# Recurrence gates as two tiles on row halves of the tensor array

## Chip, cores and metric

The kernel runs on one NeuronCore of a Trainium2 chip. What counts is the device time of one execution in microseconds (us). Before the change the median of three runs was 2362.04 us (2358.81 to 2364.02).

## The reference

Two layers over 1024 latent tokens and 256 context tokens of width 1024. Each layer normalises and modulates its input, projects it (`w_in`) and runs three branches of width 512: windowed attention, a Conformer convolution of 31 taps, and a recurrence (RG-LRU) in both directions. Each branch is multiplied by a SiLU gate, projected by `w_branch`, weighted by a sigmoid gate (`w_gate`), summed, and projected by `w_out`; a norm closes the layer. The change touches the recurrence's two gates only:

```python
def block_diag_linear(x, w, b):            # w: (8 blocks, 64, 64)
    xb = x.reshape(x.shape[:-1] + (LRU_BLOCKS, LRU_BLOCK_DIM))
    return jnp.einsum('btnd,nde->btne', xb, w).reshape(x.shape) + b

def rglru_inputs(x, w_a, b_a, w_x, b_x, lam):
    r = jax.nn.sigmoid(block_diag_linear(x, w_a, b_a))
    i = jax.nn.sigmoid(block_diag_linear(x, w_x, b_x))
    log_a = -LRU_C * r * jax.nn.softplus(-lam)
    a = jnp.exp(log_a)
    u = jnp.sqrt(-jnp.expm1(2.0 * log_a)) * i * x
    return a, u
```

## The kernel before

Channels lie on partitions and tokens along the free axis. Every product keeps fp32 accuracy by splitting both operands into a rounded part and a rest (`split`: a copy on ACT, a subtraction on DVE) in the type fp32r, and summing three products: high by high, high by low, low by high. Tokens come in three stretches: the context (256) and two halves of the latent tokens (512 each). In the gates of the recurrence the context stretch is 260 wide.

`phase1` does everything up to the gated branch outputs, `phase2` the branch and output projections and the norm. In `phase1` nine generators run as streams: `lru`, `att_values`, `att_scores`, `lru_in`, `lru_out`, `att_proj`, `att_out`, `conv` and `gates` (the `w_gate` products, not the gates of the recurrence). A `Driver` merges them: each `yield` ends a stage and names the engine that the next one needs and a condition; the driver keeps an estimated clock for PE, ACT and DVE, fed by `pe_cost` (columns of a product, whatever its rows), `act_cost` and `dve_cost`, and picks among the stages that should be ready by priority. `lru` has priority 0 in layer 0 and 1 in layer 1. The tile framework then orders the instructions of each engine by a simulated timeline and sets the waits.

For each of four blocks of 128 channels `lru_in` loads the gate weights (lines 588 to 595), makes the input projection, and splits the weights. A block of 128 channels is two of the reference's blocks of 64, so a gate's 64x64 matrices stand on the diagonal of a 128x128 tile that a memset on POOL has filled with zeros. Two directions and two gates make a tile of 128x512. In `lru`, for each channel block and direction, `taps` makes the short convolution on DVE, `parts` splits it into `xh` and `xl`, and `gate(dr, gi)` (lines 640 to 650) runs one gate: for each stretch three products over all 128 rows into one bank of PSUM, and one tanh on ACT with the bias column out of `drv`. The two gates are two stages. Then come `decay`, `drive`, `root` and `scan`. When the second direction of the last block begins, `state["late"]` lets `att_scores` start.

Banks for products come from a pool of four (`psum`); `pl_` counts those that the other streams' products hold, and lets at most three be held while the recurrence runs. The gates of the recurrence are not counted there. Wide products of `gates` use a second pool (`psum2`) until the recurrence has ended.

`load_params` and `derive_params` bring the biases to columns: `drv` holds 0.5 times the bias, columns 0 to 7 for the first gate and 8 to 15 for the second, by direction and channel block.

Of the kernel before, what the change touches and what calls it, by code (L numbers as in the profile page):

```python
# [35 lines left out]
NS, NHF, NW, NWL, NXP, NYY = 10, 14, 4, 2, 7, 6  # L36
LH = 6

# Orders the merged streams, by phase and by layer.
LEAD = (2.0, 3.0, 1.5, 2.0)  # L40
SLACK = (1.0, 5.0, 2.0, 2.0)
MARGIN = (1.0, 3.0, 1.5, 0.0)
# [7 lines left out]


class Meter:
    """An engine, with an estimate of the time that the instructions given to it take."""

    def __init__(self, eng, cost):
        self.eng, self.cost, self.t = eng, cost, 0.0
# [46 lines left out]


class Driver:
    """Merges streams of work into one order for each engine: a stage goes out when what it waits for should be there."""

    def __init__(self, pe, act, dve):
        self.phase = 0
# [1 line left out]
        self.t = dict(pe=0.0, act=0.0, dve=0.0)  # L111

    def side(self, fn):
        """Work that waits for nothing but a load."""
        was = {e: m.t for e, m in self.eng.items()}
        r = fn()
        end = self.t["pe"]
        for e, m in self.eng.items():
            d = m.t - was[e]
            if d:  # L120
                self.t[e] = max(self.t[e], min(self.t["pe"] + 2.0, self.t[e] + 2.0)) + d
                end = max(end, self.t[e])
            m.t = was[e]
        return r, end
# [19 lines left out]
        return nxt  # L144

    def run(self, gens, prio, until=None, live=()):
        """Runs the streams to their end, or to that of one of them, and returns those that are left."""
        live = list(live)
        for i, g in enumerate(gens):
            s = dict(gen=g, kind="pe", ready=self.t["pe"], prio=prio[i], cond=None)  # L150
            if self.advance(s, next(g, None)):
                live.append(s)
        while live and (until is None or any(s["gen"] is until for s in live)):
            open_ = [s for s in live if s["cond"] is None or s["cond"]()]
            assert open_, "every stream waits"
            tp = self.t["pe"]
            pick = None
            side = [s for s in open_ if s["kind"] != "pe" and self.t[s["kind"]] < tp + LEAD[self.phase]
                    and s["ready"] < max(tp, self.t[s["kind"]]) + SLACK[self.phase]]
            if side:  # L160
                pick = min(side, key=lambda s: s["prio"])
            else:
                main = [s for s in open_ if s["kind"] == "pe"]
                now = [s for s in main if s["ready"] + MARGIN[self.phase] <= tp]
                if now:
                    pick = min(now, key=lambda s: s["prio"])
                else:
                    pick = min(open_, key=lambda s: (max(s["ready"], self.t[s["kind"]]), s["prio"]))
            if not self.advance(pick, self.step(pick)):
                live.remove(pick)  # L170
        return live
# [18 lines left out]
def kernel(  # L190
# [51 lines left out]
    xs_d = DR.tile([T, D], F32, tag="xs", name="xs_d")  # L242

    P_ADA, P_GATE, P_CB, P_CG, P_CLB, P_LCW, P_LCB, P_BA, P_BX, P_LAM = 0, 24, 48, 52, 56, 60, 92, 100, 108, 116
    prm, cwt, drv = [], [], []

    def load_rows(l, get):
        ra, rb = get(), get()
# [29 lines left out]
    def derive_params(l):  # L278
        p = prm[l]
        d = K.tile([128, 64], F32, tag=f"drv{l}", name=f"drv{l}")  # L280
        dve.tensor_scalar(out=d[:, 0:16], in0=p[:, P_BA:P_BA + 16], scalar1=0.5, scalar2=None, op0=ALU.mult)
        dve.tensor_scalar(out=d[:, 16:40], in0=p[:, P_GATE:P_GATE + 24], scalar1=0.5, scalar2=None, op0=ALU.mult)
        dve.tensor_scalar(out=d[:, 40:48], in0=p[:, P_CG:P_CG + 8], scalar1=0.5, scalar2=None, op0=ALU.mult)
        t = SM.tile([128, 48], F32, tag="sp", name="sp_t")
        y, e, sx, s2, r, ny = (t[:, 8 * i:8 * i + 8] for i in range(6))
        dve.tensor_scalar(out=y, in0=p[:, P_LAM:P_LAM + 8], scalar1=-1.0, scalar2=None, op0=ALU.mult)
        dve.tensor_tensor(out=ny, in0=p[:, P_LAM:P_LAM + 8], in1=y, op=ALU.max)
        act.activation(out=e, in_=ny, func=AF.Exp, scale=-1.0)
        dve.tensor_scalar(out=r, in0=e, scalar1=2.0, scalar2=None, op0=ALU.add)
        dve.reciprocal(out=r, in_=r)  # L290
        dve.tensor_tensor(out=sx, in0=e, in1=r, op=ALU.mult)
        dve.tensor_tensor(out=s2, in0=sx, in1=sx, op=ALU.mult)
        dve.tensor_scalar(out=r, in0=s2, scalar1=1.0 / 19, scalar2=1.0 / 17, op0=ALU.mult, op1=ALU.add)
        for k in (15, 13, 11, 9, 7, 5, 3, 1):
            dve.tensor_tensor(out=r, in0=r, in1=s2, op=ALU.mult)
            dve.tensor_scalar(out=r, in0=r, scalar1=1.0 / k, scalar2=None, op0=ALU.add)
        dve.tensor_tensor(out=r, in0=r, in1=sx, op=ALU.mult)
        dve.tensor_scalar(out=y, in0=y, scalar1=0.0, scalar2=None, op0=ALU.max)
        dve.scalar_tensor_tensor(out=r, in0=r, scalar=2.0, in1=y, op0=ALU.mult, op1=ALU.add)
        dve.tensor_scalar(out=d[:, 48:56], in0=r, scalar1=-4.0, scalar2=None, op0=ALU.mult)  # L300
        dve.tensor_scalar(out=d[:, 56:64], in0=r, scalar1=4.0, scalar2=None, op0=ALU.mult)
        drv.append(d)

    sink = K.tile([128, DEPTH * NH], F32, tag="sink", name="sink")
# [4 lines left out]
    wlive = [0]  # L309

    class Wt:
        """A unit of weights, split into two parts; held from its load to its last product."""

        def __init__(self, src, a, b):
            wlive[0] += 1
# [45 lines left out]
    ada = {}  # L361

    def ada_fin(l, jjs, ps, rows, r):
        """Rows of ada, still in PSUM, to its columns, with the bias."""
        n = len(jjs) * 128
        act.activation(out=r[0:rows, 0:n], in_=ps[0:rows, 0:n], func=AF.Copy)
        for i in range(len(jjs)):
# [8 lines left out]
            dve.tensor_scalar(out=dst, in0=dst, scalar1=0.25, scalar2=None, op0=ALU.mult)  # L376

    def ada_pair(l, jj, row):
        """Two columns of ada, in three of the four products of the parts and the fourth."""
        ws = [Wt(w_ada[l][i * 512:i * 512 + 512, jj * 128:jj * 128 + 256].rearrange("(k p) n -> p k n", p=128), 4, 256)  # L380
              for i in range(2)]
        ps = psum()
        for k in range(KD):
            for v in range(2):
                pe.matmul(out=ps[0:4, 0:256], lhsT=csr[:, k, :], rhs=ws[k // 4][v][:, k % 4, :],
                          start=(k == 0 and v == 0), stop=(k == KD - 1 and v == 1))
        ada_fin(l, [jj, jj + 1], ps, 4, row)
        for w in ws:
            w.free()
# [99 lines left out]
                norm_x(*v)  # L489

    class Pool_:
        """Counts what is held of a pool, in the order of emission."""

        def __init__(self, n):
            self.n, self.used = n, 0
# [14 lines left out]
    def phase1(l, R, RH):  # L510
# [11 lines left out]
        def half(name, dt=F32):  # L522
            return RH.tile([128, 512], dt, tag="h", name=name, bufs=NHF)
# [58 lines left out]
        def lru_in():  # L582
            for cc in range(4):
# [1 line left out]
                w = wcols(w_in[l], O_XL + cc * 128)  # L585
                sl.take()
                hl_.take(3)
                lw_raw = half("lw_raw")
                pool.memset(lw_raw, 0.0)
                for dr in range(2):  # L590
                    for gi, wsrc in enumerate((lru_w_a, lru_w_x)):
                        o = (dr * 2 + gi) * 128
                        for e in range(2):
                            sp.dma_start(out=lw_raw[64 * e:64 * e + 64, o + 64 * e:o + 64 * e + 64],
                                           in_=wsrc[l, dr, 2 * cc + e])
                X = slot("X")
                for a, e in ((0, XL_C), (XL_C + C, XL_L), (XL_L + S, XW)):
                    pool.memset(X[:, a:e], 0.0)
# [6 lines left out]
                    yield from gemm_nt(w, nt, evac)  # L605
                w.free()
                yield "act"
                lwh, lwl = half("lwh", F32R), half("lwl", F32R)
                split(lw_raw, lwh, lwl)
                hl_.give()  # L610
                lws[cc] = (lwh, lwl)
# [2 lines left out]
        def lru():  # L614
            for cc in range(4):
# [17 lines left out]
                    v["xh", dr], v["xl", dr] = slot("xh", F32R)[:, 0:CW], slot("xl", F32R)[:, 0:CW]  # L633
                    split(v["xc", dr], v["xh", dr], v["xl", dr])

                def gate(dr, gi):
                    dst = v["AI"[gi], dr] = slot("AI"[gi])[:, 0:CW]
                    b = gi * 8 + dr * 4 + cc
                    wo = (dr * 2 + gi) * 128
                    for ti, t0, n in allt:  # L640
                        o, n = (0, CL) if ti == 0 else (CL + t0 - C, n)
                        ps = psum()
                        for j, (a, r) in enumerate(((lwh, "xh"), (lwh, "xl"), (lwl, "xh"))):
                            pe.matmul(out=ps[:, 0:n], lhsT=a[:, wo:wo + 128], rhs=v[r, dr][:, o:o + n], start=(j == 0),
                                      stop=(j == 2))
                        act.activation(out=dst[:, o:o + n], in_=ps[:, 0:n], func=AF.Tanh, scale=0.5, bias=d[:, b:b + 1])

                def decay(dr):
                    i = dr * 4 + cc
# [29 lines left out]
                parts(0)  # L679
                yield ("pe", sl.room(2))  # L680
                sl.take(2)
                gate(0, 0)
                yield "pe"
                gate(0, 1)
                sl.give(2)
                yield ("dve", sl.room())
                sl.take()
# [18 lines left out]
                sl.give(3)  # L706
                yield ("pe", sl.room(2))
                sl.take(2)
                gate(1, 0)
                yield "pe"  # L710
                gate(1, 1)
                hl_.give(2)
                sl.give(2)
                yield ("act", sl.room(2))
# [406 lines left out]
    def phase2(l, R, RH):  # L1121
# [175 lines left out]
                done.add(ti)  # L1297

        def hdst(ti):
            """Whether there is room for what the next layer takes in."""  # L1300
            return ti in done if ti == 0 else hq.room()() and (ti == 1 or 1 in done and 2 in done)

        def norm():
# [131 lines left out]
```

## Time and profile before

| | |
|---|---|
| median of three runs | 2362.04 us |
| span of the profiled execution | 2360.6 us |
| PE busy | 2300.4 us, 97% |
| weight loads (PEld) busy | 1931.6 us, 82% |
| DVE busy | 1762.1 us, 75% |
| ACT busy | 1063.9 us, 45% |
| POOL busy | 88.1 us, 4% |
| DMA moved | 309.94 MB, 131 GB/s |
| granted TensorE clock, mean | 0.993 of 2.4 GHz |

The profile is one execution. A product's recorded time is longer than its share of the engine, since products follow each other before the one ahead has ended; the starts in the timeline show the pace. Names such as `ps<-xh,lwh` give the output and the operands; `128*128` are rows and columns of weights in use, then follow the shape that streams through and the count. The gate products of the recurrence are those with `lwh` or `lwl`.

### The profile page before, as it was taken

The page shows a single profiled execution, that of the slowest core. Times are in us where ns is not written, and L with a number is a line of the kernel's source. Part 1 is how long each engine was busy: PE and PEld are TensorE (multiplying, and loading weights), DVE is VectorE, ACT ScalarE, POOL GpSimd, SP SyncE. Part 2 cuts the span into 40 slices and gives each one's busy share as a digit, 9 for nine tenths or more (in the row PEclk, how much of TensorE's full clock was granted, in tenths as well). Part 3 has the DMA queues.
Part 4 walks back from the last instruction along what each step waited for, and adds up shares of the span by engine and source line. Part 5 has one row for each costly group of instructions (what it writes and reads, how often), then busy time and mean ns, then how long its engine had stood idle before and what let it go on. Part 6 is the DMA issues. An engine that isn't in the chain of part 4 may idle for free.

```text
span 2360.6 us, 32714 instructions
## 1 busy us (share of the span) xinstructions
PE 2300.4 (97%) x12477; PEld 1931.6 (82%) x12477; DVE 1762.1 (75%) x2589; ACT 1063.9 (45%) x1702; POOL 88.1 (4%) x135
## 2 busy tenths in 40 slices
PE   7999999999999999999999999999999999999998
PEld 3888888878888887888888888888888878778988
DVE  5579868758969775448888839979687887667786
ACT  4555453245444565323445535555343456443231
POOL 1000000000000011000101000000000011000000
PEclk8999999999999999999999999999999999999999
DMA  7222324433344223466565521223433334338482
GB/s 276 68 74 96 116 76 132 135 102 105 96 134 126 88 87 99 169 226 215 176 210 184 188 60 61 83 90 130 134 96 95 98 95 129 119 128 273 136 274 73
DMA packets 305821, 309.94 MB, mean 131 GB/s; under 512 B 20608, under 2 KB 239616, under 8 KB 305664
## 3 DMA queue, kind: packets, MB, share of 16 engines
q1 hardware_dynamic: 277152, 255.94, 34.2%
q10 hardware_dynamic: 28512, 51.92, 6.1%
q8 instruction: 98, 1.61, 0.3%
q14 instruction: 59, 0.48, 0.1%
HBM read 232.92 MB, written 74.87 MB: 130 GB/s over the span
## 4 chain that ended last, share of the span: by engine, by line
PE 89%; DVE 4%; ACT 3%; DMA 2%; issue 1%; SPq 0%; POOLq 0%; POOL 0%; ACTq 0%; DVEq 0%
PE ps L73 82%; PE yp L73 3%; PE pt L73 2%; PE pa L73 1%; DVE wlo L73 1%; ACT whi L73 1%; DMA thl<-th 1%; DVE mx L73 0%; DMA qd<-qd 0%; DMA raw<-in_w_ada_dram 0%; DVE xp L73 0%; DVE pl L73 0%; PE p L73 0%; DMA raw<-in_w_in_dram 0%; DVE P L73 0%
## 5 line engine op out<-in xcount | busy, mean ns | idle before, releaser
L73 PE MATMUL ps<-hlhi,whi 128*128 128x512 f32 x1728 | 682.8, 396 | 4.6 <-ACT tg L73 2.1
L73 PE MATMUL ps<-hllo,whi 128*128 128x512 f32 x1728 | 678.5, 393 | 0.1
L73 PE MATMUL ps<-hlhi,wlo 128*128 128x512 f32 x1728 | 676.3, 392 | 1.1 <-DVE wlo L73 1.1
L73 ACT ACTIVATE whi<-raw 128x1024 fp32r<-128x1024 f32 x240 | 253.8, 1059 | 454.8 <-PE ps L73 425.8
L73 DVE TENSOR_TENSOR wlo<-raw,whi 128x1024 fp32r<-128x1024 f32 x240 | 293.4, 1223 | 143.0 <-ACT whi L73 142.3
L73 PEld LDWEIGHTS ps<-hlhi,whi 128*128 128x128 f32 x1728 | 325.3, 188 | 71.5 <-ACT tg L73 3.5
L73 PEld LDWEIGHTS ps<-hlhi,wlo 128*128 128x128 f32 x1728 | 325.1, 188 | 70.5 <-DVE wlo L73 2.0
L73 PEld LDWEIGHTS ps<-hllo,whi 128*128 128x128 f32 x1728 | 325.5, 188 | 63.7 <-issue 0.7
L73 DVE SCALAR_TENSOR_TENSOR acc<-u,cwt,acc 128x1296 f32<-128x1296 f32 (+1 forms) x240 | 342.1, 1426 | 2.2
L73 PE MATMUL ps<-yh,whi 128*128 128x512 f32 (+1 forms) x480 | 177.8, 377 | 8.5 <-DVE thl L73 6.5
L73 PE MATMUL ps<-yl,whi 128*128 128x512 f32 (+1 forms) x480 | 178.1, 373 | 1.5 <-DVE yl L73 1.5
L73 PE MATMUL ps<-yh,wlo 128*128 128x512 f32 (+1 forms) x480 | 179.0, 374 | 0.0
L73 ACT ACTIVATE ph<-pt 128x512 fp32r<-128x512 f32 x160 | 94.3, 594 | 162.2 <-PE pt L73 158.3
L73 DVE TENSOR_REDUCE mx<-ps 128x1 f32<-128x640 f32 (+2 forms) x144 | 104.6, 744 | 62.3 <-PE ps L73 61.8
L73 PE MATMUL ps<-whi,hlhi 128*128 128x256 f32 x512 | 144.3, 284 | 0.0
L73 PE MATMUL ps<-wlo,hlhi 128*128 128x256 f32 x512 | 144.0, 283 | 0.0
L73 ACT ACTIVATE P<-ps,nm 128x640 f32<-128x640 f32 (+2 forms) x144 | 104.9, 733 | 85.9 <-DVE nm L73 82.0
L73 DVE TENSOR_TENSOR pl<-pt,ph 128x512 fp32r<-128x512 f32 x160 | 108.7, 684 | 46.7 <-ACT ph L73 44.3
L73 PE MATMUL ps<-whi,hllo 128*128 128x256 f32 x512 | 142.6, 283 | 0.0
L73 PE MATMUL ps<-hchi,whi 128*128 128x256 f32 x480 | 138.1, 288 | 3.6 <-ACT rstd L73 1.2
L73 PE MATMUL ps<-hchi,wlo 128*128 128x256 f32 x480 | 137.4, 286 | 0.0
L73 PE MATMUL ps<-hclo,whi 128*128 128x256 f32 x480 | 136.5, 285 | 0.0
(203 smaller groups left out, 3829.1 us busy)
## 6 DMA issues: line engine op xcount, KB each, us to landing
raw<-in_w_in_dram SPq DMA_DIRECT2D x60, 512.0 KB
raw<-in_w_branch_dram SPq DMA_DIRECT2D x60, 512.0 KB
raw<-in_w_ada_dram SPq DMA_DIRECT2D x48, 512.0 KB
raw<-in_w_gate_dram SPq DMA_DIRECT2D x48, 512.0 KB
th<-tg ACTq DMA_DIRECT2D x96, 256.0 KB
thl<-th SPq DMA_DIRECT2D x96, 256.0 KB
raw<-in_w_out_dram SPq DMA_DIRECT2D x40, 512.0 KB
yd<-gs ACTq DMA_DIRECT2D x48, 256.0 KB
```

The lines of the kernel that those rows point to most:

```text
L73: return f(*a, **k)
```

## The change

A gate weight tile is 128x256 without zeros: the rows are the two blocks of 64 input channels, and for each direction 64 columns of the first gate stand beside 64 of the second. Each half of the rows is a tile of its own (`tile_position`), 64 rows by 128 columns, and gives both gates of its 64 channels into a bank of its own. One call of `gates_of` does both gates of a direction and yields after each stretch. Four tanh of 64 partitions bring a stretch from two banks to the tiles `A` and `I`; two of them move between partition halves. For these a bias tile `gbt` holds the first gate's biases on the first 64 partitions and the second's on the others, filled by four small copies a layer. The four weight loads of a channel block are 128x64, and the memset is gone. The program is built with 4096 bytes of DMA scratch. Comments and docstrings that the diff also removes are left out here.

```diff
-    prm, cwt, drv = [], [], []
+    prm, cwt, drv, gbs = [], [], [], []
...
+        gbt = K.tile([128, 16], F32, tag=f"gbt{l}", name=f"gbt{l}")
+        for e in range(2):
+            r = slice(64 * e, 64 * e + 64)
+            for gi in range(2):
+                dve.tensor_copy(gbt[64 * gi:64 * gi + 64, 8 * e:8 * e + 8], d[r, 8 * gi:8 * gi + 8])
+        gbs.append(gbt)
         drv.append(d)
...
-                lw_raw = half("lw_raw")
-                pool.memset(lw_raw, 0.0)
+                lw_raw = half("lw_raw")[:, 0:256]
                 for dr in range(2):
                     for gi, wsrc in enumerate((lru_w_a, lru_w_x)):
-                        o = (dr * 2 + gi) * 128
-                        for e in range(2):
-                            sp.dma_start(out=lw_raw[64 * e:64 * e + 64, o + 64 * e:o + 64 * e + 64],
-                                           in_=wsrc[l, dr, 2 * cc + e])
+                        o = (dr * 2 + gi) * 64
+                        sp.dma_start(out=lw_raw[:, o:o + 64],
+                                     in_=wsrc[l, dr, 2 * cc:2 * cc + 2].rearrange("e i o -> (e i) o"))
...
-                lwh, lwl = half("lwh", F32R), half("lwl", F32R)
+                lwh, lwl = half("lwh", F32R)[:, 0:256], half("lwl", F32R)[:, 0:256]
...
-                def gate(dr, gi):
-                    dst = v["AI"[gi], dr] = slot("AI"[gi])[:, 0:CW]
-                    b = gi * 8 + dr * 4 + cc
-                    wo = (dr * 2 + gi) * 128
+                def gates_of(dr):
+                    dst = [slot(g)[:, 0:CW] for g in "AI"]
+                    v["A", dr], v["I", dr] = dst
+                    wo = dr * 128
                     for ti, t0, n in allt:
                         o, n = (0, CL) if ti == 0 else (CL + t0 - C, n)
-                        ps = psum()
+                        pss = [psum() for _ in range(2)]
                         for j, (a, r) in enumerate(((lwh, "xh"), (lwh, "xl"), (lwl, "xh"))):
-                            pe.matmul(out=ps[:, 0:n], lhsT=a[:, wo:wo + 128], rhs=v[r, dr][:, o:o + n], start=(j == 0),
-                                      stop=(j == 2))
-                        act.activation(out=dst[:, o:o + n], in_=ps[:, 0:n], func=AF.Tanh, scale=0.5, bias=d[:, b:b + 1])
+                            for e in range(2):
+                                rows = slice(64 * e, 64 * e + 64)
+                                pe.matmul(out=pss[e][:, 0:n], lhsT=a[rows, wo:wo + 128], rhs=v[r, dr][rows, o:o + n],
+                                          start=(j == 0), stop=(j == 2), tile_position=(64 * e, 0))
+                        for e in range(2):
+                            b = 8 * e + dr * 4 + cc
+                            for gi in range(2):
+                                rows = slice(64 * gi, 64 * gi + 64)
+                                act.activation(out=dst[gi][64 * e:64 * e + 64, o:o + n], in_=pss[e][rows, 0:n], func=AF.Tanh,
+                                               scale=0.5, bias=gbs[l][rows, b:b + 1])
+                        yield "pe"
...
-                gate(0, 0)
-                yield "pe"
-                gate(0, 1)
+                yield from gates_of(0)
...
-                gate(1, 0)
-                yield "pe"
-                gate(1, 1)
+                yield from gates_of(1)
...
-    nc = _bacc.Bacc("TRN2", target_bir_lowering=False, num_devices=1)
+    nc = _bacc.Bacc("TRN2", target_bir_lowering=False, num_devices=1, dynamic_dma_scratch_size=4096)
```

## Rows read from the trace of the kernel before

**Rows 1.** The page: head, part 1 (busy us, share), part 4 (chain).
```profile
span 2360.6 us, 32714 instructions
...
PE 2300.4 (97%) x12477; PEld 1931.6 (82%) x12477; DVE 1762.1 (75%) x2589; ACT 1063.9 (45%) x1702; POOL 88.1 (4%) x135
...
PE 89%; DVE 4%; ACT 3%; DMA 2%; issue 1%; SPq 0%; POOLq 0%; POOL 0%; ACTq 0%; DVEq 0%
```

**Rows 2.** Groups by form, gates: count | busy us, mean ns | idle before.
```profile
L73 PE MATMUL ps<-xh,lwl 128*128 128x512 f32 x64 | 25.2, 394 | 0.0
...
L73 ACT ACTIVATE A<-ps,drv 128x512 f32<-128x512 f32 x32 | 21.5, 690 | 15.1 <-PE ps L73 15.1
...
L73 PE MATMUL ps<-xl,lwh 128*128 128x260 f32 x32 | 9.0, 282 | 0.0
...
L73 ACT ACTIVATE A<-ps,drv 128x260 f32<-128x260 f32 x16 | 7.6, 476 | 30.1 <-PE ps L73 30.1
```

**Rows 3.** Timeline of PE, gate products: start us, us recorded, instruction.
```profile
113.14 0.28 PE L73 MATMUL ps<-xh,lwh 128*128 128x260 f32 x1
113.26 0.29 PE L73 MATMUL ps<-xl,lwh 128*128 128x260 f32 x1
...
113.97 0.40 PE L73 MATMUL ps<-xh,lwl 128*128 128x512 f32 x1
114.20 0.40 PE L73 MATMUL ps<-xh,lwh 128*128 128x512 f32 x1
```

**Rows 4.** Busy us by stretch: length, PE, PEld, DVE, ACT, POOL; clock; DMA.
```profile
1500.00:1660.00 160.00, 158.81 (x738) 132.13 (x737) 134.82 (x131) 88.03 (x104) 1.01 (x8) 1.00 0.34 110
...
1900.00:2110.00 210.00, 199.67 (x1007) 160.36 (x1006) 148.54 (x256) 116.72 (x219) 17.00 (x14) 0.98 0.34 109
```

**Rows 5.** Timeline of weight loads, two places.
```profile
105.71 0.19 PEld L73 LDWEIGHTS ps<-hchi,wlo 128*128 128x128 f32 x1
105.81 0.19 PEld L73 LDWEIGHTS ps<-hchi,whi 128*128 128x128 f32 x1
...
113.14 0.19 PEld L73 LDWEIGHTS ps<-xl,lwh 128*128 128x128 f32 x1
```

**Rows 6.** Timeline of PE, into ada's product on 4 rows.
```profile
104.85 0.28 PE L73 MATMUL ps<-hchi,whi 128*128 128x256 f32 x1
104.97 0.28 PE L73 MATMUL ps<-hclo,whi 128*128 128x256 f32 x1
105.18 0.27 PE L73 MATMUL ps<-sel,arow 4*128 4x2 f32 x1
```

**Rows 7.** Timeline of ACT, the eviction that makes its operand.
```profile
100.44 0.35 ACT L73 ACTIVATE arow<-ps 4x256 f32<-4x256 f32 x1
```

**Rows 8.** Timeline of PE, out of the product on 4 rows.
```profile
105.53 0.25 PE L73 MATMUL ps<-sel,arow 4*128 4x2 f32 x1
105.71 0.39 PE L73 MATMUL ps<-hchi,wlo 128*128 128x256 f32 x1
105.93 0.28 PE L73 MATMUL ps<-hchi,whi 128*128 128x256 f32 x1
```

**Rows 9.** Timeline of PE, the first and last of 57 runs of gate products.
```profile
107.74 0.37 PE L73 MATMUL ps<-xh,lwh 128*128 128x260 f32 x1
...
1629.52 0.39 PE L73 MATMUL ps<-xh,lwl 128*128 128x512 f32 x1
```

**Rows 10.** Timeline of PE, a run of three between other products.
```profile
297.22 0.40 PE L73 MATMUL ps<-xh,lwh 128*128 128x512 f32 x1
...
297.91 0.39 PE L73 MATMUL ps<-hllo,whi 128*128 128x512 f32 x1
```

**Rows 11.** The page, part 3: queue, kind, packets, MB, share of engines.
```profile
q1 hardware_dynamic: 277152, 255.94, 34.2%
q10 hardware_dynamic: 28512, 51.92, 6.1%
q8 instruction: 98, 1.61, 0.3%
q14 instruction: 59, 0.48, 0.1%
```

## The prediction

> **What bounds the kernel now.** I read the page first. PE is busy 97% of a span of 2360.6 us and carries 89% of the chain that ended last [rows 1]; no other engine is near. The median of the three timed runs, 2362.04 us, lies 1.4 us above that span; I take this 1.4 us as what lies around it and add it at the end. Busy PE is not PE at its peak, because the ends of matmuls are modelled, so I go by the distance from one start to the next. The groups by form give the gate products: 64 of 512 columns and 32 of 260 for each of three kinds of product, 288 in all [rows 2]. Their recorded 390 and 280 ns overlap: in the timeline the next 512-column product starts 0.23 us later and the next 260-column one 0.12 us later [rows 3]. So the price is 192 x 0.232 + 96 x 0.119 = 44.5 + 11.4 = 56 us, all of it inside the stretches with the recurrence. In one of these PE is busy 158.8 of 160 us [rows 4], so time taken from PE there comes off the end, as long as PE stays full afterwards.
>
> **The change, part by part.**
>
> *Products.* The number of matmuls stays: a direction had 2 gates x 3 stretches x 3 products = 18 and has 3 stretches x 3 products x 2 halves = 18, with the same columns. What can be saved is that the two halves run at the same time. If each of the 144 pairs takes what one product takes, half of 56 us goes: 28.0 us. If the halves run one after the other, nothing goes. The trace has no pair of row tiles, so these are the two ends. I take the pair as side by side: the halves share no row, and each has a bank of its own.
>
> Two bounds for a pair follow from the weight loads. Each product brings a load of 128 columns; two loads in a row start 0.10 to 0.11 us apart when nothing else holds them [rows 5]. If the loads of the two halves also overlap, they cost nothing extra. If they share one path, a pair needs 2 x 0.108 = 0.216 us of loading: hidden under a 512-column pair (0.232), but not under a 260-column pair (0.119), whose gain falls from 0.119 to 0.022 us. The saving is then 96 x 0.232 + 48 x 0.022 = 23.3 us. I take the loads as overlapping.
> The Trainium skill ("TensorE: Matmul & The Clock Gate", Part 3) says that a weight load overlaps matmuls in flight only where its rows differ from theirs. The trace disagrees on the first half of that: the load for the product at 113.26 starts at 113.14, together with the previous product on the same 128 rows [rows 3, 5]. On the second half it speaks for loads of two row halves overlapping, and with its 4 ns between the starts of two tiles, an estimate, the 28.0 us would be 144 x 0.004 = 0.6 us less. No run here shows it.
>
> *Changing the row size.* This term speaks against the change. The kernel already has one product on fewer rows: ada's little selection matmul, 4 rows. Before it, a 256-column product is followed after 0.21 us instead of 0.12 [rows 6]; its operand had been ready since 100.8 [rows 7], so this is no data wait: 0.09 us going in. Coming out, the last 4-row product (normal step 0.11) is followed after 0.175, 0.065 too much, and the first 128-row product then takes 0.22 instead of 0.12 [rows 8], since its weights were loaded only from 105.71 on and not beside its predecessor [rows 5]: 0.105 more. The first step inside is 0.02 longer. Sum for one round trip: 0.09 + 0.02 + 0.065 + 0.105 = 0.28 us. For 64 rows the row may understate it: the first load inside may be exposed in full (+0.09, 0.37), and with a single load path the second half's too (+0.107, 0.48). Below, 0 if a half-array change needs no emptying. I take 0.28, the measured row.
>
> How often? After each stretch the generator yields, and its next stage is due only once four evictions are through by the model, so other streams' products come between: 16 direction-blocks x 3 = 48 round trips at least. The order is also cut finer than the stages: the gate products of today, 32 stages, lie in 57 separate runs, the first a single product at 107.74 and the last ending at 1629.5 [rows 9], because xl is late or a bank is not free; many cuts lie at a stretch's end [rows 10], which will be a stage's end anyway. If every stage is cut at today's rate there are 85. I take 60. Cost: 60 x 0.28 = 17.0 us (ends 0 and 85 x 0.48 = 41).
>
> *Banks.* A stage now needs two of four banks at once. Where one is free, one half runs through alone and nothing is saved. A stretch that stands alone, as the three products from 297.22 to 297.91 [rows 10], may say that this happens; I take 12% of the pairs: 28.0 becomes 24.6 us.
>
> *Evictions.* 96 evictions on 128 partitions become 192 on 64. Duration goes by columns (0.69 us for 512, 0.48 for 260 [rows 2]), so ACT gets 64 x 0.69 + 32 x 0.476 = 59 us more. ACT is busy 55% in the densest such stretch [rows 4], so most hides beside PE. What stays visible: a bank is held for up to 4 x 0.69 = 2.8 us. I take 1.5 us of PE waiting over 48 stages (ends 0 and 48 x 0.5 = 24, were every stage to wait most of one eviction).
> The Trainium skill ("TensorEngine Tiling", PSUM Bottleneck) warns that tiling speeds up the products and not the emptying of PSUM. Here that would need ACT to be the bound: 59 us more over both layers, where one window of 160 us alone leaves ACT 72 us free [rows 4], is no bound, so by these rows it takes part only through held banks.
>
> *A longer recurrence chain.* Six more evictions (3.7 us) and one more hop for each of 8 direction-blocks (5 us together, an estimate) put the end of the recurrence in a layer some 8 x 5 = 40 us later, and attention with it. In layer 1 less fill is then left for the attention tail, where PE stands idle 10.3 of 210 us, 5% [rows 4]: 40 x 0.05 = 2 us (ends 0 and 10, the tail's idle time once more).
>
> *The rest at nothing.* Gate weights half as wide: 8 splits on ACT and DVE are halved, by some 0.3 us each (half of an operation on 512 columns [rows 2]), the memset goes and eight loads become four; all run well ahead of the first product, and if that cover were gone they would be worth 8 x 0.7 = 5.6 us at most, as a gain. The eight little copies of biases sit beside the first layer's products and inside filler. The smaller DMA scratch serves queues of a kind that the page does not list: its four are hardware-dynamic or instruction fetch [rows 11], so zero.
>
> *Sum.* -24.6 + 17.0 + 1.5 + 2.0 = -4.1 us: 2360.6 - 4.1 = 2356.5, and with the 1.4 us around it 2358 us.
>
> **Rivals.**
> *Cheap changes (faster).* Going to half the rows empties nothing, or costs only the two bubbles of 0.09 and 0.065: 60 x 0 to 0.155 = 0 to 9.3 us instead of 17. Then -24.6 + 9.3 + 3.5 = -11.8 to -21.1 us: 2341 to 2350. For it: halves stay in their own rows, loads could go ahead. Against it: the 4-row product shows the bubbles each time it comes.
> *One load path (slower).* Loads of both halves queue behind each other. Saving 23.3 x 0.88 = 20.5; round trip 0.28 + 0.107 = 0.39, x 60 = 23.4; with 3.5 for banks and tail: +6.4 us, 2368. It decides from some 44 blocks on (44 x 0.39 = 17.2 against 20.5 - 3.5 = 17.0). For it: loads never come closer than about 0.11 us in the trace.
> *The halves take turns (the change doesn't do what it says; slower).* No pair overlaps: 17.0 + 3.5 = +20.5 us, 2382.5. For it: nowhere in the trace are two products under way on different rows. Against it: separate rows and banks.
>
> **How the numbers follow.** Forecast 0.46, own range 2351 to 2366; cheap changes 0.22; one load path 0.19; taking turns 0.13. What can be told from no change here is about 0.2%, 4.7 us: 2357.3 to 2366.8. Faster: 0.22 and 0.36 of the forecast's 0.46 (0.17) = 0.39. Same: 0.26 of the forecast and a third of one load path (0.06) = 0.32. Slower: the remaining 0.03 of the forecast, 0.13 of one load path and 0.13 = 0.29. The range from 2342 to 2377 leaves out the halves that take turns and the cheapest changes.
>
> **What would show it.** Two gate products starting within some 10 ns of each other, and the next pair 0.23 us later (loads hidden); 0.12 us per 260-column pair for overlapping loads, 0.22 for one path. The step into a block of halves 0.09 over normal and the first full product after it 0.17 over. 48 to 85 such blocks; more gives back the saving. PE's idle in the tail of layer 1's attention over 10 us would show the longer chain. The planner counts a product by its columns alone, so it sees none of the saving and gives PE's work out as before. I am wrong if pairs start one product apart, if no bubble stands at the borders, or if the merged order of the streams moves more time outside the recurrence than inside it.

## The result, and the profile after

The change made the kernel slower: 2427.74 us (median; 2427.09 to 2430.69) against 2360.43 us for the kernel before, run beside it. The ratio is 1.0283, 95% interval 1.0271 to 1.0296, some 67 us. The forecast was 2358 us with a range of 2342 to 2377. The page and the view by core of the changed kernel:

```profile
span 2426.4 us, 32847 instructions
...
PE 2336.0 (96%) x12477; PEld 1925.6 (79%) x12477; DVE 1763.8 (73%) x2597; ACT 1130.4 (47%) x1798; POOL 86.0 (4%) x127
...
PE 84%; DVE 7%; ACT 3%; DMA 2%; issue 2%; SPq 0%; POOL 0%; POOLq 0%; ACTq 0%; DVEq 0%
```
```profile
core 0: 2426.4 us, clock 0.982
```

Against [rows 1], PE has as many products but is busy 36 us longer and idle 30 us longer, and its share of the chain fell from 89% to 84% in favour of DVE (4% to 7%). ACT has 66 us more. The mean granted clock fell from 0.993 to 0.982. The clock has only its two levels here, 2.4 and 1.2 GHz, so this is (1 - 0.982) x 2426 - (1 - 0.993) x 2361 = 43.7 - 16.5 = 27 us of full-speed work lost; part of it falls into PE's idle time and costs nothing. While busy, PE spent 63.5 us at 1.2 GHz against 22.0 before: (63.5 - 22.0) / 2 = 21 us.

Where it went is seen in stretches, cut at the last scan of a layer's recurrence, at the end of its attention and at the first and last branch products. Columns as in [rows 4]; first the kernel before, then the changed one:

```profile
75.00:376.00 301.00, 300.52 (x1596) 253.77 (x1595) 228.92 (x245) 160.79 (x203) 2.44 (x18) 1.00 0.29 91
376.00:917.00 541.00, 528.50 (x3021) 444.91 (x3020) 424.49 (x663) 251.06 (x493) 17.75 (x18) 1.00 0.36 112
917.00:1033.00 116.00, 114.52 (x588) 96.93 (x587) 48.12 (x70) 38.59 (x60) 4.16 (x6) 1.00 0.43 143
...
1375.00:1648.00 273.00, 271.81 (x1284) 227.30 (x1283) 221.95 (x202) 146.99 (x177) 1.31 (x11) 1.00 0.26 84
1648.00:2125.00 477.00, 466.03 (x2315) 380.06 (x2314) 355.13 (x557) 218.25 (x405) 17.16 (x16) 0.99 0.35 112
```
```profile
75.00:417.00 342.00, 332.27 (x1686) 265.36 (x1685) 233.69 (x259) 197.28 (x256) 0.54 (x9) 0.98 0.27 86
417.00:954.00 537.00, 517.80 (x2912) 433.74 (x2911) 425.88 (x659) 254.92 (x494) 22.73 (x24) 0.98 0.35 108
954.00:1072.00 118.00, 117.18 (x607) 99.18 (x606) 41.47 (x63) 32.33 (x55) 0.29 (x3) 1.00 0.46 147
...
1412.00:1730.00 318.00, 310.41 (x1430) 245.72 (x1429) 246.56 (x229) 186.06 (x234) 0.66 (x10) 0.98 0.26 86
1730.00:2189.00 459.00, 440.26 (x2178) 356.23 (x2178) 332.37 (x530) 210.44 (x395) 18.29 (x16) 0.98 0.34 107
```

PE's idle time, length less busy, rose in both recurrences from 0.5 and 1.2 to 9.7 and 7.6 us, and in both attentions, which hold no gate product, from 12.5 and 11.0 to 19.2 and 18.7 us. All four have a mean clock of 0.98. Work moved between stretches too: the recurrence now has more products in it and attention fewer. So half of the new idle time is where the change alters no instruction.

The tiles themselves do what they say. A timeline of PE with a stretch whose halves run side by side (x2: two starts merged into one row):

```profile
200.72 0.39 PE L73 MATMUL ps<-hllo,whi 128*128 128x512 f32 x1
201.04 0.50 PE L73 MATMUL ps<-xh,lwh 64*128 64x512 f32 x2
201.38 0.40 PE L73 MATMUL ps<-xl,lwh 64*128 64x512 f32 x2
201.61 0.40 PE L73 MATMUL ps<-xh,lwl 64*128 64x512 f32 x2
201.93 0.50 PE L73 MATMUL ps<-hlhi,wlo 128*128 128x512 f32 x1
202.27 0.40 PE L73 MATMUL ps<-hlhi,whi 128*128 128x512 f32 x1
```

In each of these pairs the second product starts 10 ns after the first, and the next pair 0.23 us later, as one full product after another in [rows 3]. Against that pace the first step, 200.72 to 201.04, is 0.09 us too long, the step after it 0.105, the step out (201.61 to 201.93) 0.09 and the one after it 0.11: 0.39 us a round trip. What is left of a gain: from the last product before to the second after, less their usual steps, ten undisturbed runs of three pairs took 0.96 us where full rows take 1.10. But 31 runs in the changed kernel are a lone half of three products, as this one:

```profile
147.73 0.39 PE L73 MATMUL ps<-hlhi,wlo 128*128 128x512 f32 x1
148.05 0.49 PE L73 MATMUL ps<-xh,lwh 64*128 64x512 f32 x1
148.38 0.39 PE L73 MATMUL ps<-xl,lwh 64*128 64x512 f32 x1
148.61 0.39 PE L73 MATMUL ps<-xh,lwl 64*128 64x512 f32 x1
148.93 0.50 PE L73 MATMUL ps<-hlhi,whi 128*128 128x512 f32 x1
149.26 0.39 PE L73 MATMUL ps<-hllo,whi 128*128 128x512 f32 x1
```

They took 1.08 us where full rows take 0.64, and there are two to a stretch. Of the 144 times that a product of one half could have one of the other half beside it, only 78 came about; in 74 of these it was the same product of the other half.

With that PE's time adds up. Counted in the same way, 61 of the 66 runs, those at 2.4 GHz and without a wait over 0.2 us, took 60.4 us where full rows take 46.2 at the prices of the prediction: the products that were to save time cost 14 us more. With 30 us of idle time and 21 us for the lower clock these are 65 of the 66 us by which the span grew.

Evictions take as long on 64 partitions as on 128 in [rows 2] (0.69 us for 512 columns), and there are twice as many. Groups by form after:

```profile
L73 ACT ACTIVATE I<-ps,gbt 64x512 f32<-64x512 f32 x64 | 43.9, 686 | 1.0
L73 ACT ACTIVATE A<-ps,gbt 64x512 f32<-64x512 f32 x64 | 43.7, 684 | 45.8 <-PE ps L73 45.0
...
L73 PE MATMUL ps<-xl,lwh 64*128 64x260 f32 x32 | 6.7, 350 | 4.2 <-DVE xl L73 4.2
```

The list of PE's waits (total us, times, longest) has the recurrence's inputs, the softmax of attention and the splits before its value products on it:

```profile
PE ps L73 <- ACT P L73: 9.5, 6, 3.2
PE yp L73 <- DVE pl L73: 7.5, 7, 2.4
...
PE ps L73 <- DVE xl L73: 4.2, 2, 2.6
PE ps L73 <- ACT arow L73: 4.0, 3, 2.3
...
PE ps L73 <- ACT xh L73: 3.7, 1, 3.7
```

In the kernel before the waits of `ps` on `xl`, `xh` and `arow` are missing from this list.

### The profile page after: what moved, and what is told of

The parts are those of the page before. It is cut to its first block, busy times and chain, and to the rows that moved or that the text cites. A ratio compares the mean times of both kernels' runs of the same rounds, so it can differ in the third digit from the quotient of the medians.

```text
span 2426.4 us, 32847 instructions
## 1 busy us (share of the span) xinstructions
PE 2336.0 (96%) x12477; PEld 1925.6 (79%) x12477; DVE 1763.8 (73%) x2597; ACT 1130.4 (47%) x1798; POOL 86.0 (4%) x127
## 4 chain that ended last, share of the span: by engine, by line
PE 84%; DVE 7%; ACT 3%; DMA 2%; issue 2%; SPq 0%; POOL 0%; POOLq 0%; ACTq 0%; DVEq 0%
PE ps L73 78%; PE yp L73 3%; PE pt L73 2%; DVE acc L73 2%; PE pa L73 1%; DVE wlo L73 1%; DMA thl<-th 1%; DMA raw<-in_w_ada_dram 1%; DVE pl L73 1%; ACT whi L73 1%; DVE mx L73 0%; DVE xp L73 0%; ACT A L73 0%; DVE P L73 0%; PE p L73 0%
## 5 line engine op out<-in xcount | busy, mean ns | idle before, releaser
L73 DVE TENSOR_TENSOR pl<-pt,ph 128x512 fp32r<-128x512 f32 x160 | 109.0, 687 | 71.4 <-ACT ph L73 70.0
```

Source lines behind the costliest of these rows:

```text
L73: return f(*a, **k)
```

## The experiments

Three things change at once: the form of the products, the number of evictions, and the order in which the planner merges the streams, since it is told other stages and other costs. Each run below has one or two of them. "The old plan" means that the planner is given the stages and costs of before by force; the framework's own ordering on each engine, which works from a simulated timeline, can still react. It did: of the 12189 products outside the gates some 900 (e1, e5, e6) or 1600 (e9, e10) stand elsewhere in PE's list than before, against 6239 in the change and 6277 in e13. Times are medians; "before" was 2361.1 to 2361.8 us beside these runs.

| run | products | evictions a stretch | plan | us | ratio (95%) |
|---|---|---|---|---|---|
| before | full rows | 2 | old | 2361 | |
| e5 | full rows | 4 | old | 2379.5 | 1.0083 (1.0066 to 1.0100) |
| e6 | tiles | 2 | old | 2381.7 | 1.0087 (1.0072 to 1.0102) |
| e1 | tiles | 4 | old | 2401.6 | 1.0169 (1.0154 to 1.0184) |
| e10 | tiles, all paired | 2 | old | 2366.6 | 1.0030 (1.0014 to 1.0045) |
| e9 | tiles, all paired | 4 | old | 2388.9 | 1.0120 (1.0105 to 1.0135) |
| e13 | full rows | 2 | three stages | 2406.0 | 1.0189 (1.0174 to 1.0204) |
| e2 | full rows | 2 | three stages, told 4 evictions | 2406.2 | 1.0188 (1.0173 to 1.0204) |
| the change | tiles | 4 | three stages, told 4 | 2427.7 | 1.0283 (1.0271 to 1.0296) |
| e14 | tiles, paired | 4 | three stages, true costs | 2401.2 | 1.0165 (1.0148 to 1.0182) |

**e1, tiles in the old plan.**

```diff
-                        yield "pe"
...
+                    for part in (allt[:2], allt[2:]):
+                        counted(lambda: [stretch(*nt) for nt in part], 3 * 1284 / 2400.0, 3 * 0.143 + 1284 / 1200.0)
+                        if len(part) == 2:
+                            yield "pe"
```

`stretch` is the body of the loop over stretches. `counted` runs it and moves the planner's clocks of PE and ACT by the times given, here those of before. The splits of the gate weights and the bias copies are told as before too.

> Tiles on row halves and four evictions a stretch as in the change, but the planner is given the stages and the costs of the kernel before (two stages a direction: context and first half, then second half; product and eviction times as if the block-diagonal products ran), so that the streams are merged as before. Theory O (the merged order is what costs: PE waits for ACT and DVE elsewhere, and falls to half clock after such waits): 2350 to 2375 us, PE waits over 1 us near the 43 us of before. Theory P (the products themselves cost: changes of row size, halves that run alone, half clock brought on by half-filled products): 2400 us or more.

2401.6 us, between the two. The order outside the recurrence did come back: attention's windows have PE idle for 12.3 and 11.9 us, as in the kernel before. Its two windows:

```profile
390.00:930.00 540.00, 527.75 (x3011) 443.76 (x3010) 424.93 (x664) 251.41 (x493) 17.81 (x18) 1.00 0.37 114
1686.00:2161.00 475.00, 463.10 (x2302) 377.76 (x2302) 353.23 (x554) 217.13 (x403) 17.18 (x16) 0.99 0.35 111
```

So these 40 us come from inside the recurrence, and neither theory holds alone. PE's waits over 1 us add up to 52 us, against 35 before by the same count. One wait stands out in the timeline of PE; the row below it is ACT's, of the copy that PE waits for:

```profile
1482.80 0.39 PE L73 MATMUL ps<-hlhi,wlo 128*128 128x512 f32 x1
1494.25 1.01 PE L73 MATMUL ps<-xh,lwh 64*128 64x260 f32 x4 [11.06 <-ACT xh L73]
...
1492.92 1.27 ACT L73 ACTIVATE xh<-xc 128x1284 fp32r<-128x1284 f32 x1 [14.30 <-DVE xc L73]
```

PE takes its instructions in order, and the gate product stands where its input should have been there. PE stands for 11 us, and nothing behind it on PE can start. ACT is not the engine that is behind at this moment: it has stood idle for 14.3 us itself. Both wait for DVE, which is busy without a break over that time and whose list has the four operations of `xc` (the short convolution of the next channel block) in between `acc` (of `conv`), the scan and other work. In the kernel before the copy of the same block starts at 1464.3, and PE does not wait. ACT was behind one direction earlier: there the copy `xh` starts 9.5 us after its input is there (1.6 us before the change), with the first direction's gate evictions, twelve where there were six, and its decay ahead of it on ACT.

**e2, full rows in the new plan.**

```diff
+                    for nt in allt:
+                        n = CL if nt[0] == 0 else nt[2]
+                        counted(lambda: stretch(*nt), 6 * n / 2400.0, 4 * (0.143 + n / 1200.0))
+                        yield "pe"
```

Here `stretch` makes both gates of a stretch on full rows, with two evictions.

> Block-diagonal products of before on all 128 rows with one eviction per gate and stretch, but merged as the change merges: both gates of a stretch in one stage, three stages a direction, and the planner told of four evictions a stretch. Theory O: 2400 to 2440 us though no product has 64 rows. Theory P: 2355 to 2370 us.

2406.2 us: without one product on 64 rows and without one eviction more, the order alone costs 45 us, as theory O had it.

**e3, the DMA scratch alone.** The edit is the last line of the diff.

> The kernel before with nothing but the smaller DMA scratch; every engine's order is unchanged. Both theories: no change, 2357 to 2366 us.

2362.1 us, ratio 0.9999 (0.9990 to 1.0008): no change.

**e4, a stage held back until two banks are free.**

```diff
-                        yield "pe"
+                        yield "pe" if ti == 2 else ("pe", lambda: pl_.used <= 2)
...
-                yield ("pe", sl.room(2))
+                yield ("pe", both(sl.room(2), lambda: pl_.used <= 2))
```

> The change, with a stage of the gates held back until the other streams hold at most two of the four banks, so that the halves of a stretch find two banks and run side by side. Theory P with halves that run alone as the cost: 2370 to 2400 us. Theory O: the merged order is another one again and the time lands anywhere from 2370 to 2430 us, with the gate products themselves some 10 us shorter than in the change.

2430.7 us. The condition never held a stage back: PE's order is that of the change, so this is the change run again. It says that lone halves do not come from the planner's count of banks, and neither theory is tested.

**e5, twice the evictions, full rows, old plan.**

```diff
-    act.activation(out=dst[:, o:o + n], in_=ps[:, 0:n], ...)
+    was = act.t
+    for e in range(2):
+        q = slice(64 * e, 64 * e + 64)
+        act.activation(out=dst[q, o:o + n], in_=ps[q, 0:n], ...)
+    act.t = was + 0.143 + n / 1200.0
```

> The kernel before, block-diagonal products and its planner's stages and costs, but each gate eviction as two on 64 partitions (96 more on ACT, 59 us by the durations of before). Theory E (the doubled evictions make ACT and DVE late against the order, and PE waits for the next gate's input): 2385 to 2405 us, as with the tiles in the old plan, with a PE wait of several us before a gate product. Theory P (the tiles' own cost, row-size changes and lone halves): 2360 to 2370 us.

2379.5 us: 18 us, between the two. The wait is there (the row is of PE's waits, total, times and longest):

```profile
PE ps L73 <- ACT xh L73: 7.0, 2, 4.9
```

Of these, 4.9 us stand before the same gate product as the 11 us in e1, and there too ACT itself has been idle, for 8.1 us, until DVE has `xc` ready.

**e6, tiles with one eviction a bank, old plan.** Beside e1's lines:

```diff
-    for gi in range(2):
-        act.activation(out=dst[gi][64 * e:64 * e + 64, o:o + n], in_=pss[e][rows, 0:n], ...)
+    act.activation(out=dst[e][:, o:o + n], in_=pss[e][:, 0:n], ...)
```

> Tiles in the plan of before with one eviction per bank on all 128 partitions (two a stretch); the gates' values then land in the wrong places, which leaves the moving of two quarters out. Theory E: 2345 to 2368 us, since only the evictions cost. Theory P: 2385 to 2400 us.

2381.7 us: 20 us, between the bands, near theory P. With e5's 18 this makes 38 of the 40 us of e1: the two nearly add up. About 7 of the 20 us are the gate products' own time: in 53 of 56 runs they took 56.1 us where full rows take 49.0. What the 20 also hold is another division of the work: the old kernel's two stages are the two gates, here they are the context with the first half, and the second half. Full rows in this division were not run.

**e9 and e10, both halves in one buffer of two banks.** Beside e1's lines; e10 has e6's too:

```diff
-    pss = [psum() for _ in range(2)]
+    both_ = psum2()
+    pss = [both_[:, 512 * e:512 * e + 512] for e in range(2)]
```

> As the tiles in the old plan (2401.6 us), but the two halves of a stretch take one buffer of two banks from the pool of the wide products, so both halves find their banks together and all 144 pairs should run side by side. If lone halves are the larger part of the tiles' own cost (a run of three lone products took 1.08 us where three full ones take 0.64): 2385 to 2395 us. If the order moves more than the pairs do: anywhere from 2390 to 2430 us, with the gate products nevertheless shorter.

> The same with one eviction per bank (the gates' values land in the wrong places). From the tiles with two evictions (2381.7 us) less some 12 us for lone halves: 2360 to 2375 us. That is the best that tiles can give in the old plan; under 2357 would say that tiles pay once halves are paired and evictions are not doubled.

All 144 pairs ran together, in 41 and 45 runs. With four evictions 2388.9 us, with two 2366.6: both are in the first band given, and lone halves had cost 13 and 15 us. The gate products' own time bears this out: from e6 to e10 it goes from 7 us over full rows to 7.5 under (42.4 us where full rows take 49.9, in 42 of 45 runs). The two versions differ in one more thing: in e9 and e10 the gates take nothing from the four banks of the other streams. What is left in e10 is a loss of 5 us (3 to 11 by the interval), though the gate products are 7.5 us shorter. In its profile PE is idle for 71.4 us against 60.2, and busy at 1.2 GHz for 38 us against 22, which costs another 8: so the gain, and more, is given back in waits and after them.

**e7, e8, e12 and e11: another order, the same instructions.**

```diff
+    act.t += 0.143 + n / 1200.0                  # e7: the planner counts each gate eviction twice
-HOP = (0.2, 0.4, 0.1, 0.15)
+HOP = (0.25, 0.4, 0.15, 0.15)                    # e8; e11 on the changed kernel
+HOP = (0.15, 0.4, 0.05, 0.15)                    # e12
```

> The kernel before in all instructions; only the planner counts each gate eviction twice. Theory O (the order before is a favourable one, and any other order of the same work costs): 2375 to 2410 us with not one more instruction. Theory E: 2358 to 2370 us.

> The kernel before in all instructions; the planner's wait between the stages of a stream is 0.05 us longer in the two first phases, a change without meaning for the work. Theory O: 2375 to 2410 us. If the order before is not special: 2355 to 2368 us.

> The kernel before in all instructions, with that wait 0.05 us shorter. If 2361 is a favourable order among ordinary ones: 2375 to 2420 us. If the longer wait was a special mishap: 2357 to 2368 us.

> The change, with the planner's wait between stages 0.05 us longer in the first phases, which took the kernel before from 2361.8 to 2419.7 us. If the order before was a favourable one and the change's is an ordinary one: within 25 us of 2428 to either side. If the change has a cost that no order gives back: 2420 us or more.

e7 2373.3, e8 2419.7, e12 2409.8 us (ratios 1.0054, 1.0245, 1.0204), e11 2440.6 us. The kernel before loses 12, 58 and 49 us when an estimate in its planner is shifted, with nothing else changed. Its order is a favourable one among these three neighbours. e7 falls between its bands, e8 even above the one of theory O, e12 into the first; e11 fits both of its sentences and decides nothing. How far the order moves does not say what it costs: 6051 of the products outside the gates stand elsewhere in e7 and 5469 in e8. The windows of attention in e8 show PE idle for 27.0 and 16.3 us where before has 12.5 and 11.0:

```profile
382.00:906.00 524.00, 497.00 (x2785) 413.18 (x2784) 403.70 (x643) 240.24 (x476) 12.51 (x18) 0.97 0.35 109
...
1701.00:2178.00 477.00, 460.70 (x2278) 374.67 (x2277) 343.36 (x547) 213.69 (x401) 17.94 (x16) 0.99 0.35 111
```

The changed kernel moved by 13 us under the same shift, from 2427.7 to 2440.6.

**e13, three stages, costs as before.** The edit is e2's, with two evictions told instead of four.

> Block-diagonal products and two evictions a stretch, in three stages a direction (both gates of one stretch each), with the planner told their true number of evictions and the costs of before. If the finer stages make the new order slow: 2390 to 2410 us, near the 2406 us of stages and told evictions together. If the told evictions do: 2362 to 2375 us.

2406.0 us, as e2, though half of PE's list is ordered otherwise than there: the told evictions are not needed for the 45 us. PE, ACT and DVE have the instructions of the kernel before, one for one, in another order. Its two attentions, columns as above:

```profile
397.00:923.00 526.00, 501.14 (x2824) 418.08 (x2823) 402.75 (x643) 243.97 (x482) 16.46 (x21) 0.98 0.35 107
...
1716.00:2170.00 454.00, 435.64 (x2164) 354.65 (x2163) 332.33 (x536) 209.67 (x395) 17.99 (x16) 0.98 0.35 109
```

PE is idle there for 24.9 and 18.4 us, where it was 12.5 and 11.0. Over the whole span it is idle 26 us longer than before, and busy at 1.2 GHz for 57 us against 22, 18 us of full-speed work: with that the 45 us are accounted for. That it is the third stage as such which costs them is not shown: they lie within the 12 to 58 us that a shift without meaning costs.

**e14, paired halves and true costs for the planner.**

```diff
+    was = pe.t, act.t
+    both_ = psum2()
+    pss = [both_[:, 512 * e:512 * e + 512] for e in range(2)]
...
+    pe.t, act.t = was[0] + 3 * n / 2400.0 + 0.39, was[1] + 4 * (0.17 + n / 1000.0)
```

> The change with paired halves (one buffer of two banks) and a planner that is told half the product time plus 0.39 us a stage for the change of row size, and evictions of 0.68 us. If wrong prices keep the change from a good order: 2370 to 2400 us. If any order but the one of before costs: 2405 to 2440 us, though the gate products are some 15 us shorter than in the change.

2401.2 us: 26 us better than the change, just above the first of the two bands. Pairing may explain about half of it (13 us in e9); whether the rest is the true prices or another throw of the order these runs do not tell. No version beat the kernel before.

## Why the prediction was wrong

- *"Time taken from PE there comes off the end, as long as PE stays full afterwards."* This step failed. The sum had no term for the merged order, which the last sentence of the prediction named and priced at nothing. It measures 45 us by itself (e2, e13). A planner that merges nine streams by estimated clocks answers another division into stages with another order of everything, attention included, and PE, which takes its list in order, waits in it. The step fails without a new plan too: in e10 the gate products take 7.5 us less of PE, and the time is 5 us longer. The sign given at the end, more time moved outside the recurrence than inside, was near: 14.5 us of PE's new idle time lie in the attentions, 15.6 in the recurrences.
- *Evictions.* Priced at 1.5 us of PE waiting with an upper end of 24; measured 18 us on full rows (e5), 20 to 22 with the tiles (e1 against e6, e9 against e10). The argument "ACT is busy 55%" was the wrong view. It is an average, and the recurrence is a chain through DVE and ACT: in e1 the copy `xh` of a block's second direction starts 1.2 to 9.9 us after its input is there, where it was 4.1 us at most, with the doubled evictions of the first direction ahead of it on ACT. PE does not wait there but later, before the next block's gate, for DVE and with ACT idle (e1, e5). That the lateness on ACT brings about that wait fits the traces, and no run shows it step by step.
- *Banks.* Priced at 12% of the pairs; 66 of 144, 46%, did not come about, and a lone half costs 0.44 us over full rows besides. So the term for products and changes of row size, forecast at -24.6 + 17.0 = -7.6 us, came out at some +14. Pairing them gave 13 to 15 us back (e9, e10).
- *Changing the row size.* Forecast 0.28 us in 60 places (16.8 us; the 17.0 is a slip that moves nothing), measured 0.39 in 66. The mechanism of [rows 6, 8] held to the step; the part taken at 0.02, the first load inside, is exposed in full (0.105), as the upper end had it.
- *Products side by side, loads overlapping.* Right: 10 ns between the starts of 512-column halves (mostly 3 to 4 ns for 260 columns, and for both in e9 and e10), 0.23 us to the next pair, 0.12 for 260 columns, and the weight loads of both halves 10 ns apart where the products are. The rivals "one load path" and "taking turns" fell. What was said for the first, that loads never come closer than about 0.11 us, misread the trace: [rows 5] has 0.10, and two loads for the product `ps<-ident,pj` at 265.7 start 0.056 us apart. "Cheap changes" fell with the 0.39 us.
- *The longer chain.* Layer 0's last scan starts at 417 instead of 376 us, 41 us later where 40 were forecast. The match is luck: with the same evictions in the old plan it starts at 390 (e1), and with none more in the new one at 397 (e13). That this costs only 5% of itself did not hold: attention in layer 1 was idle 7.8 us longer, and it is not told apart here from the order.
- *Scratch and weight loads at nothing.* Right for the scratch (e3). The weight loads were not tried alone.

Tiles (20) and evictions (18 to 20) add up to 38 to 40 in the old order, and the new order costs 45 alone, but all three together cost 67 and not 83 to 85. That part of the extra work fills waits which the new order has anyway would explain it; it is not shown. How much of the 67 us belongs to each cause in the new plan is therefore open, and so is which decision of the planner makes its order slow. The sizes of 5 to 20 us are no larger than what a shift of the order costs, and the old plan is not quite the old order; only for the pairing does the gate products' own time on PE give the same number.

## What to carry to other kernels

When a kernel's order comes from a planner with estimated costs, an edit that changes a stage, a cost or a buffer changes the order of everything. Before pricing the edit, ask what the order is worth: run the old kernel with a meaningless nudge to the planner, and measure the edit with the planner's inputs held fixed, then the planner's inputs with the edit left out. Halving the products of an engine that is 97% busy bought nothing here: the stage around them runs through DVE and ACT and got twice the evictions, and even without these (e10) the time did not fall. Tiles on fewer rows save time on the array only where both halves run together and the run is worth more than the 0.39 us at its borders: three pairs of 512 columns took 1.09 us where full rows take 1.39, three pairs of 260 columns 0.75 where they take 0.71.

## What the hardware showed that I had not expected

A fall of the clock without a long wait. In the changed kernel the granted clock was 0.5 (1.2 GHz) for 3.4 us from 194.3, and no two starts in the 8 us before lie more than 0.57 us apart; the falls in the kernel before, past its first 60 us and up to its last product, all have two starts 1.27 us or more apart just before them. What PE had done was full products, products with 4 columns of weights in use, a mixed run of tiles, ada's products on 4 rows and this lone half (timeline of PE):

```profile
193.03 0.49 PE L73 MATMUL ps<-xh,lwh 64*128 64x512 f32 x1 [0.25 <-ACT I L73]
193.37 0.39 PE L73 MATMUL ps<-xl,lwh 64*128 64x512 f32 x1
193.60 0.39 PE L73 MATMUL ps<-xh,lwl 64*128 64x512 f32 x1
194.01 0.56 PE L73 MATMUL ps<-hlhi,whi 128*128 128x512 f32 x1
194.37 0.63 PE L73 MATMUL ps<-hllo,whi 128*128 128x512 f32 x1
194.80 0.63 PE L73 MATMUL ps<-hlhi,wlo 128*128 128x512 f32 x1
```

From 194.37 on a 512-column product takes 0.43 us instead of 0.23. It happened once in this profile; the other falls of the changed kernel, between the same bounds, come at or just after steps of 1.8 to 4.1 us from one start to the next. It is no accident of one execution: in e4, where PE has the same list, the clock falls at 195.3, three products further on in it and again with no step over 0.57 us before.
